# Extra matrix products into fresh PSUM banks ahead of the recurrence's pairwise products and the feed-forward's first feature tile

## The chip, the cores and the metric

The kernel runs on one NeuronCore of a Trainium2 chip. The metric is the device time of one execution in microseconds (us). The engines in the text are TensorE (PE in the profile; its weight loads are PEld), VectorE (DVE), ScalarE (ACT), GpSimd (POOL) and SyncE (SP, which only issues transfers here).

## The reference: one step of a two-layer hybrid encoder

There are 1152 tokens of width 1024: one prompt of 1024 tokens and eight samples of 16 tokens. Everything is f32.

- Layer 0: RMS norm with adaptive shift and scale, then an RWKV-7 time mixing with 16 heads of 64. The recurrence is, per head and token, `S = S*w + (S a) b^T + v k^T`, `y = S r`. Then a SwiGLU feed-forward with 2816 features: `(silu(h Wg) * (h Wu)) Wd`.
- Layer 1: norm, attention of each 64-token chunk to itself and the eight chunks before it, then the same kind of feed-forward.

Outputs are the activations of all tokens, the recurrence's states and the shared keys and values.

## The kernel before

Activations lie with features on the partitions and tokens along the free dimension. A dense product in high precision is three products of a reduced f32 type (fp32r): the operand is split into a high part (ScalarE copy, L268) and a low part (VectorE subtraction, L269), and `mm3` (L271) issues high by high, high by low and low by high. Each product by `mm` (L138) goes through L139, so in the profile nearly all TensorE rows have that line and are told apart by their tiles. A product of two plain f32 operands is issued as two matmul instructions, one of fp32r as one.

**Layer 0's mixing.** Tokens are cut in three blocks of 384 and nine windows of 128 (`w` = 0 to 8, three for a block; window 8 holds the samples). `layer0a` (L1184) weaves the windows of block b-1 with the projections of block b (`proj_lora` at L570 among them), five steps of one to four of the other; the last three windows are woven with the output projection. `win_prep` (L813) works on one window and one half `hf` of the heads. It loads the operands XL and BK by seven transfers (BK has a single buffer, L823), and for each of two chunks `c` takes two PSUM banks `Gs` (L838, tag G, two banks in all) and makes eight pairwise products `G<-XL,BK`: four features by two heads `e`, head 0 on partitions 0 to 63 and head 1 on 64 to 127, each 64 rows by 128 columns of weights with 128 moving columns, head e into bank e. VectorE masks each bank into YL and XL (L845, L847). Then BK is transposed (L856) by way of two more G banks `pt` (L850) and ScalarE copies them out (L858). So one call makes 16 pairwise products and 16 transposes, and there are 18 calls. `win_first`, `win_solve`, `win_merge` and `win_state` do the triangular inverse and the recurrence, on small tiles with the tags st and Y.

**Feed-forward.** Gate and up projections use Strassen's scheme with seven products of half-size operands (`gate_up`, L1319). The tokens are two column groups: c=0 has 512 tokens and moving widths of 256, c=1 has 640 tokens and widths of 320. Product i takes the weight halves (hi, lo) from a generator, takes a wide PSUM tile of two banks (tags S, two buffers, and PT, one buffer) and issues 12 matmuls for each c. The inputs `B[c][i]` come from `strassen_in` (L1255): GpSimd combinations, ScalarE and VectorE splits. For the first of 22 feature tiles, `ffn` (L1361) calls `gate_up` for c=0 (L1365), runs what is left of `strassen_in` for c=1, and calls `gate_up` again for c=1 with the same weights (L1368). The other 21 feature tiles do both c at once (L1370). This happens in both layers.

**What sets the order.** The program text gives priorities; a scheduler that simulates the timeline (L1935) fixes, when the kernel is built, one order of instructions for each engine. At run time each engine works through its own order and waits by semaphores.

Of the kernel before, what the change touches and what calls it, by code (L numbers as in the profile page):

```python
# [137 lines left out]
def mm(nc, out, lhsT, rhs, start, stop):  # L138
    return nc.tensor.matmul(out, lhsT, rhs, start=start, stop=stop)  # L139


class Trunk:
# [631 lines left out]
    def st(self, tag, shape, bufs=1, dt=F32):  # L774
        return self.pp.tile(shape, dt, tag=tag, name=self.nm(tag), bufs=bufs)

    def win_first(self, w, hf, ld):

        nc = self.nc
        b, wi = divmod(w, 3)  # L780
        fs = slice(4 * hf, 4 * hf + 4)
        pa = self.wt("pa", [128, 2, 8, 64], 1)
        for i, n in enumerate(("kk", "b")):
            nc.sync.dma_start(pa[:, i], self.sp[b][n][:, wi, fs, :].rearrange("p f (c t) -> p (f c) t", t=64))
        G = self.bank("G", 2)
        for c in range(2):
            for f in range(4):
                for e in range(2):
                    h = slice(64 * e, 64 * e + 64)
                    mm(nc, G[h, (c * 4 + f) * 64:(c * 4 + f + 1) * 64], pa[h, 1, 2 * f + c], pa[h, 0, 2 * f + c], True, True)  # L790
        aab = self.wt("Aab", [128, 8, 64], 2)
        gv = G.rearrange("p (g t) -> p g t", t=64)
        if w == 8:
            nc.vector.tensor_tensor(aab, gv, self.C("mas").rearrange("p (o t) -> p o t", o=1).broadcast_to([128, 8, 64]), ALU.mult)
        else:
            nc.scalar.activation(aab, gv, AF.Copy)
        for e in range(2):
            nc.scalar.dma_start(ld[:, hf, e], aab[64 * e:64 * e + 64])
        return aab
# [13 lines left out]
    def win_prep(self, w, hf):  # L813

        nc = self.nc
        smp = w == 8
        b, wi = divmod(w, 3)
        fs = slice(4 * hf, 4 * hf + 4)
        R = Ctx()
        src = lambda n, p0=0, p1=128: self.sp[b][n][p0:p1, wi, fs, :].rearrange("p f (c t) -> p (f c) t", t=64)  # L820
        ring, nr = (self.st, 1) if (w, hf) == (7, 1) and 1 else (self.wt, 3)
        xl = ring("XL", [128, 3, 8, 64], nr)
        bk = self.wt("BK", [128, 8, 2, 64], 1)  # L823
        nc.sync.dma_start(xl[0:64, 0], src("kk", 0, 64))
        nc.sync.dma_start(xl[64:128, 1], src("kk", 64, 128))
        nc.sync.dma_start(bk[0:64, :, 0, :], src("b", 0, 64))
        nc.sync.dma_start(bk[64:128, :, 0, :], src("k", 64, 128))
        nc.sync.dma_start(bk[0:64, :, 1, :], src("k", 0, 64))
        nc.sync.dma_start(bk[64:128, :, 1, :], src("b", 64, 128))
        nc.sync.dma_start(xl[:, 2], src("r"))  # L830
        R.eend = self.eends[b][:, fs, 2 * wi:2 * wi + (8 if smp else 2)]
        bkv = bk.rearrange("p (f c) s t -> p f c (s t)", c=2)

        yl = ring("YL", [128, 2, 2, 4, 64], nr)
        mr = self.C("mrs" if smp else "mr").rearrange("p (o t) -> p o t", o=1).broadcast_to([128, 4, 64])
        ma = self.C("mas" if smp else "ma").rearrange("p (o t) -> p o t", o=1).broadcast_to([128, 4, 64])
        for c in range(2):
            Gs = [self.bank("G", 2) for _ in range(2)]  # L838
            for f in range(4):
                for e in range(2):  # L840
                    h = slice(64 * e, 64 * e + 64)
                    mm(nc, Gs[e][:, f * 128:(f + 1) * 128], bkv[h, f, c], xl[h, e:3:2 - e, 2 * f + c, :], True, True)
            for e in range(2):
                gv = Gs[e].rearrange("p (f x t) -> p f x t", f=4, x=2)
                nc.vector.tensor_tensor(yl[:, c, e], gv[:, :, 1, :], mr, ALU.mult)  # L845
                h2 = slice(64 * (1 - e), 64 * (1 - e) + 64)
                nc.vector.tensor_tensor(xl[h2, e, c::2], gv[h2, :, 0, :], ma[h2], ALU.mult)  # L847

        bkt = ring("BKT", [128, 2, 2, 256], nr)
        pt = [self.bank("G", 2) for _ in range(2)]  # L850
        for c in range(2):
            for f in range(4):
                for e in range(2):
                    o0 = (c * 4 + f) * 64
                    h = slice(64 * e, 64 * e + 64)
                    nc.tensor.transpose(pt[e][:, o0:o0 + 64], bkv[h, f, c], self.C("ident")[h, h])  # L856
        for e in range(2):
            nc.scalar.activation(bkt[:, :, e], pt[e].rearrange("p (c f d) -> p c (f d)", c=2, f=4), AF.Copy)  # L858
        R.xl, R.yl, R.bkt, R.TT = xl, yl, bkt, self.TT.pop((w, hf))
        uv = R.uv = self.wt("UV", [128, 2, 2, 4, 64], 3)  # L860
        for c in range(2):
            for e in range(2):
                p0 = 64 * (1 - e)
                nc.sync.dma_start(uv[p0:p0 + 64, c, e], self.sv[b][wi, c * 64:(c + 1) * 64, e, 4 * hf:4 * hf + 4, :])
        return w, hf, R
# [450 lines left out]
        yield put(a21)  # L1316
        yield put(a22)

    def gate_up(self, sd, B, W, cs):  # L1319

        nc = self.nc
        dve = nc.vector
        gp = nc.gpsimd
        n0, n1 = 256 * cs[0], 576 if cs[-1] else 256
        new = (lambda: self.halfraw()[:, :n1]) if n1 == 256 else (lambda: self.ev("t")[:, n0:n1])

        def product(i):
            hi, lo = next(W)
            t = self.wide()[:, 256:832]
            for c in cs:  # L1330
                z = (t[:, 0:256], t[:, 256:576])[c]
                for k in range(4):
                    s = slice(k * 128, (k + 1) * 128)
                    self.mm3(z, hi[:, s], lo[:, s], B[c][i][0][:, k], B[c][i][1][:, k], k == 0, k == 3)
            return t[:, n0:n1]

        def add(eng, out, x, y):
            eng.tensor_tensor(out, x, y, ALU.add)  # L1338

        t1, s0, s1, t5, u2, u3 = (new() for _ in range(6))  # L1340
        nc.scalar.activation(t1, product(0), AF.Copy)
        add(dve, s0, product(1), t1)
        nc.scalar.activation(s0, s0, AF.Silu)
        nc.scalar.activation(s1, product(2), AF.Copy)
        nc.scalar.activation(t5, product(4), AF.Copy)  # L1345
        add(dve, u2, product(5), t1)
        add(gp, s1, s1, t5)
        add(gp, s1, s1, u2)
        self.silu = nc.scalar.activation(s1, s1, AF.Silu)
        add(dve, u3, product(6), u2)  # L1350
        add(gp, t5, t5, u3)
        dve.tensor_tensor(s1, s1, t5, ALU.mult)
        add(dve, u3, product(3), u3)
        dve.tensor_tensor(s0, s0, u3, ALU.mult)
        for h, s in enumerate((s0, s1)):
            for c in cs:
                o, n = 256 * c - n0, (256, 320)[c]
                t0 = 512 * c + n * h
                nc.sync.dma_start(sd[:, t0:t0 + n], s[:, o:o + n])

    def ffn(self, l, B, W, part1, xsrc, dst, done):  # L1361

        nc = self.nc
        sd = [self.dp.tile([128, 2, 1152], F32, name=f"sd{l}_{p}") for p in range(11)]
        self.gate_up(sd[0][:, 0], B, iter(W), (0,))  # L1365
        for _ in part1:
            pass
        self.gate_up(sd[0][:, 0], B, iter(W), (1,))  # L1368
        for f in range(1, 22):
            self.gate_up(sd[f // 2][:, f % 2], B, self.strassen_weights(l, f), (0, 1))  # L1370
        self.ada = self.ada_steps(range(12, 28), "acc", 1) if l == 0 else iter(())
# [2 lines left out]
        act, W = {}, {}  # L1374
# [11 lines left out]
        for p, c in [(p, c) for p in range(9) for c in range(2)] + [(9, 1), (10, 1), (9, 0), (10, 0)]:  # L1386
# [6 lines left out]
                for n in range(8):  # L1393
                    ns = slice(n % 4 * 128, (n % 4 + 1) * 128)
                    d, parts = self.pz(c)
                    for z, o, m in parts:
                        for i in range(2):
                            wh, wl = W[p][i][n // 4]
                            hi, lo = (act[p, c][h][:, i, o:o + m] for h in range(2))
# [553 lines left out]
```

## Time and profile before

| | us |
|---|---|
| three runs: median (lowest, highest) | 3859.59 (3859.28, 3872.24) |
| the profiled execution, its own time | 3864.46 |
| its span, first to last instruction | 3862.7 |
| TensorE busy in the span | 3540.6 |
| VectorE busy | 2291.8 |
| ScalarE busy | 1575.7 |
| mean granted TensorE clock | 0.932 |

Rows of the timeline read: start, duration, engine, line, operation, out<-in, weights' rows*columns, moving shape, count, and in brackets the idle time before it with what ended that. Where a row merges several instructions, the duration runs to the end of the last one. Rows of the windows view read: from:to, length, busy time of PE, PEld, DVE, ACT and POOL with their counts, granted TensorE clock (1.00 is full), mean busy share of the DMA engines, GB/s.

### The profile page before, as it was taken

The numbers are of one execution on the slowest core, as the hardware profiler recorded it, in microseconds if no ns is written. First come the engines' busy times: TensorE is split into PE (matmuls) and PEld (weight loads), VectorE is DVE, ScalarE is ACT, GpSimd is POOL, SyncE is SP. The second block draws the span as 40 slices with busy tenths as digits, with TensorE's granted clock in tenths as the row PEclk, the third lists the DMA queues.
The fourth block names the chain that finished last, engine by engine and source line by source line (L and its number), as shares of the span: only waits on it lengthen the run. The fifth ranks groups of instructions, "written<-read, shape, count | busy, mean of one in ns | idle before, by whom it ended". The sixth has DMA issues, their size and how long they took to land.

```text
span 3862.7 us, 72343 instructions
## 1 busy us (share of the span) xinstructions
PE 3540.6 (92%) x28614; PEld 3125.0 (81%) x28614; DVE 2291.8 (59%) x4420; ACT 1575.7 (41%) x2998; POOL 643.2 (17%) x564
## 2 busy tenths in 40 slices
PE   5889989989888699999999899789889799999999
PEld 4777778777666599999887879677777799999998
DVE  4666666765445764554456752666675764554567
ACT  5545646544223433333311353565654533333310
POOL 0000000000010364453000100000000254453000
PEclk8887998889798789999999999899999899999999
DMA  5775776776664412223755112454555322222521
GB/s 209 233 218 163 214 207 182 200 199 199 187 201 147 143 67 75 74 75 105 254 179 182 70 62 97 141 152 140 153 185 167 116 80 75 74 75 92 171 86 70
DMA packets 428963, 552.31 MB, mean 143 GB/s; under 512 B 128432, under 2 KB 296880, under 8 KB 424144
## 3 DMA queue, kind: packets, MB, share of 16 engines
q1 hardware_dynamic: 352640, 449.49, 36.4%
q0 software_dynamic: 21840, 79.31, 6.8%
q10 hardware_dynamic: 54144, 18.89, 2.1%
q8 instruction: 225, 3.69, 0.4%
q14 instruction: 114, 0.93, 0.1%
HBM read 413.42 MB, written 134.12 MB: 142 GB/s over the span
## 4 chain that ended last, share of the span: by engine, by line
PE 69%; DMA 9%; DVE 9%; issue 6%; ACT 5%; POOL 1%; SPq 1%; ACTq 0%; DVEq 0%; POOLq 0%
PE S L139 31%; PE PT L139 15%; PE acc L139 13%; PE st L139 3%; PE O L139 2%; PE G L139 1%; DVE h L269 1%; PE PT L1779 1%; PE aux L139 1%; DMA raw<-in_wada 1%; DMA TT<-Z 1%; DMA Z<-T 1%; DVE wlo L269 1%; PE Y L139 1%; ACT pts L1780 1%
## 5 line engine op out<-in xcount | busy, mean ns | idle before, releaser
L139 PE MATMUL S<-h,w 128*128 128x320 f32 (+1 forms) x4944 | 698.9, 300 | 18.2 <-DVE h L269 7.7
L139 PEld LDWEIGHTS S<-h,w 128*128 128x128 f32 x4944 | 676.8, 192 | 26.6 <-DVE h L269 12.8
L139 PE MATMUL acc<-mx,whi 128*128 128x384 f32 x1728 | 512.5, 374 | 41.8 <-ACT mx L268 20.2
L139 PE MATMUL S<-h,wh 128*128 128x320 f32 (+1 forms) x2844 | 529.8, 337 | 14.0 <-DVE h L1151 8.1
L139 PEld LDWEIGHTS S<-h,wh 128*128 128x128 f32 x2844 | 455.4, 189 | 70.6 <-issue 11.7
L139 PEld LDWEIGHTS acc<-mx,whi 128*128 128x128 f32 x1728 | 340.4, 205 | 74.1 <-ACT mx L268 23.9
L268 ACT ACTIVATE w<-rq 128x512 fp32r<-128x512 f32 x308 | 192.4, 629 | 503.5 <-PE S L139 203.1
L269 DVE TENSOR_TENSOR w<-rq,w 128x512 fp32r<-128x512 f32 x308 | 268.6, 875 | 199.5 <-ACT w L268 198.9
L139 PE MATMUL PT<-h,w 128*128 128x320 f32 (+1 forms) x2448 | 355.4, 300 | 14.1 <-ACT w L268 6.9
L139 PEld LDWEIGHTS PT<-h,w 128*128 128x128 f32 x2448 | 337.9, 192 | 17.8 <-ACT w L268 7.1
L139 PE MATMUL acc<-mx,wlo 128*128 128x384 f32 x864 | 318.8, 369 | 6.5 <-DVE wlo L269 6.5
L139 PE MATMUL PT<-h,wh 128*128 128x320 f32 (+1 forms) x1428 | 286.4, 344 | 10.8 <-DVE wh L269 3.9
L1338 POOL TENSOR_TENSOR t<-t,t 128x576 f32<-128x576 f32 (+1 forms) x132 | 216.5, 1641 | 417.0 <-ACT t L1345 295.3
L139 PEld LDWEIGHTS PT<-h,wh 128*128 128x128 f32 x1428 | 233.5, 190 | 41.7 <-issue 6.0
L269 DVE TENSOR_TENSOR wlo<-raw,whi 128x1024 fp32r<-128x1024 f32 x114 | 139.6, 1226 | 85.3 <-ACT whi L268 84.3
L139 PEld LDWEIGHTS acc<-mx,wlo 128*128 128x128 f32 x864 | 176.7, 205 | 16.3 <-DVE wlo L269 10.3
L269 DVE TENSOR_TENSOR h<-h,h 128x1024 fp32r<-128x1024 f32 (+4 forms) x112 | 122.9, 1111 | 89.9 <-ACT h L268 73.0
L268 ACT ACTIVATE wh<-rq 128x512 fp32r<-128x512 f32 x124 | 74.8, 625 | 242.8 <-PE S L139 160.7
L268 ACT ACTIVATE h<-h 128x1024 fp32r<-128x1024 f32 (+4 forms) x112 | 103.3, 935 | 168.1 <-DMA h<-sd 111.7
L268 ACT ACTIVATE whi<-raw 128x1024 fp32r<-128x1024 f32 x114 | 119.6, 1053 | 124.3 <-PE acc L139 78.9
L1338 DVE TENSOR_TENSOR t<-S,t 128x576 f32<-128x576 f32 (+1 forms) x116 | 86.4, 745 | 132.0 <-PE S L139 132.0
L1405 DVE TENSOR_TENSOR h<-h,S 128x640 f32<-128x640 f32 (+1 forms) x150 | 111.9, 750 | 78.8 <-PE S L139 78.7
(433 smaller groups left out, 5754.7 us busy)
## 6 DMA issues: line engine op xcount, KB each, us to landing
h<-in_wada SPq DMA_DIRECT2D x64, 512.0 KB, 6.4
rq<-in_wg SPq DMA_DIRECT2D x88, 256.0 KB, 2.6
rq<-in_wu SPq DMA_DIRECT2D x88, 256.0 KB, 2.6
rq<-in_wd SPq DMA_DIRECT2D x88, 256.0 KB, 3.0
raw<-in_wada POOLq DMA_DIRECT2D x32, 512.0 KB, 5.0
kc<-in_ck SPq DMA_DIRECT2D x16, 1024.0 KB, 5.0
vc<-in_cv SPq DMA_DIRECT2D x16, 1024.0 KB, 5.8
sd<-t SPq DMA_DIRECT2D x88, 160.0 KB, 1.9
```

The costliest lines, as they stand in the source:

```text
L139: return nc.tensor.matmul(out, lhsT, rhs, start=start, stop=stop)
L268: self.nc.scalar.activation(hi, x, AF.Copy)
L269: self.nc.vector.tensor_tensor(lo, x, hi, ALU.subtract)
L1338: eng.tensor_tensor(out, x, y, ALU.add)
L1405: nc.vector.tensor_tensor(y, y, d, ALU.add)
L1779: nc.tensor.transpose(pt[:, j * 128:(j + 1) * 128], P[:, j * 128:(j + 1) * 128], self.C("ident"))
L1780: nc.scalar.activation(pts[:, 0:nk * 128], pt[:, 0:nk * 128], AF.Copy)
```

## The change

`keep` is a new function that issues, n times, one f32 product of constants into each of two banks: 64 rows by 128 columns of weights, 512 moving columns, head half e into bank e. `win_prep` calls it for windows 0, 3 and 6: before the pairwise products of each chunk (once, in window 6 twice) into the banks `Gs`, and once before the transposes into `pt`. In `gate_up` a new argument makes each of the seven products begin with one (c=0) or three (c=1) fp32r products of the weights with themselves, 128 rows by 128 columns with 512 moving columns, into the bank of the wide tile which the product itself uses next. Only the first feature tile of each layer passes that argument. The real products that follow start their banks anew, so nothing that is computed changes.

```diff
+    def keep(self, ts, n):
+        for _ in range(n):
+            for e, t in enumerate(ts):
+                h = slice(64 * e, 64 * e + 64)
+                mm(self.nc, t, self.cst[h, 0:128], self.cst[h, 0:512], True, True)
...
         for c in range(2):
             Gs = [self.bank("G", 2) for _ in range(2)]
+            if w % 3 == 0:
+                self.keep(Gs, 1 + (w == 6))
...
         pt = [self.bank("G", 2) for _ in range(2)]
+        if w % 3 == 0:
+            self.keep(pt, 1)
...
-    def gate_up(self, sd, B, W, cs):
+    def gate_up(self, sd, B, W, cs, keep=0):
...
             hi, lo = next(W)
-            t = self.wide()[:, 256:832]
+            t = self.wide()
+            for _ in range(keep):
+                mm(nc, t[:, 512 * cs[0]:512 * cs[0] + 512], hi[:, 0:128], hi, True, True)
+            t = t[:, 256:832]
...
-        self.gate_up(sd[0][:, 0], B, iter(W), (0,))
+        self.gate_up(sd[0][:, 0], B, iter(W), (0,), 1)
         for _ in part1:
             pass
-        self.gate_up(sd[0][:, 0], B, iter(W), (1,))
+        self.gate_up(sd[0][:, 0], B, iter(W), (1,), 3)
```

That is 44 f32 products in `win_prep` (22 pairs: 6 for window 0, 6 for window 3, 10 for window 6) and 28 fp32r products in each layer's feed-forward.

## The prediction, before the run

> **What bounds the kernel now.** I read the page first, then windows of 50 us over the span, then windows of 0.1 us around each change of the granted clock, then TensorE's timeline there. From the page:
>
> ```profile
> span 3862.7 us, 72343 instructions
> PE 3540.6 (92%) x28614; PEld 3125.0 (81%) x28614; DVE 2291.8 (59%) x4420; ACT 1575.7 (41%) x2998; POOL 643.2 (17%) x564
> PEclk8887998889798789999999999899999899999999
> PE 69%; DMA 9%; DVE 9%; issue 6%; ACT 5%; POOL 1%; SPq 1%; ACTq 0%; DVEq 0%; POOLq 0%
> ```
>
> TensorE is busy for 92% of the span and carries 69% of the chain that ended last; but the clock row shows that a busy TensorE is not always a fast one. Between the edges found with the 0.1 us windows:
>
> ```profile
> 347.90:365.00 17.10, 16.96 (x60) 12.29 (x59) 16.06 (x33) 12.37 (x23) 0.53 (x1) 0.50 0.56 176
> 368.40:399.10 30.70, 29.47 (x392) 25.69 (x391) 20.17 (x42) 11.60 (x22) 1.58 (x3) 0.50 0.66 173
> 665.30:702.90 37.60, 35.94 (x154) 28.81 (x151) 31.57 (x75) 22.22 (x39) 1.05 (x2) 0.50 0.57 167
> 979.40:1016.90 37.50, 31.61 (x170) 22.38 (x168) 21.20 (x58) 7.04 (x13) 1.42 (x3) 0.50 0.65 173
> 1337.80:1375.30 37.50, 29.32 (x94) 23.30 (x95) 34.06 (x54) 18.26 (x40) 29.91 (x25) 0.55 0.11 35
> 3068.30:3082.00 13.70, 6.11 (x27) 5.82 (x28) 13.70 (x38) 11.35 (x23) 0.08 (x1) 0.50 0.00 0
> 3099.00:3110.00 11.00, 9.54 (x34) 7.90 (x35) 9.39 (x13) 1.99 (x5) 7.84 (x7) 0.53 0.00 0
> 1400.00:1450.00 50.00, 50.00 (x379) 50.00 (x378) 26.64 (x30) 16.61 (x28) 24.80 (x16) 1.00 0.21 73
> ```
>
> The third number is TensorE's busy time, the fifth VectorE's, the seventh GpSimd's, then the clock. The clock here is half or full and nothing between (0.55 is a mean over an edge). Half-clock stretches last 17.1, 30.7, 37.6 and 37.5 us, which is 5, 9, 11 and 11 times 3.41 to 3.42 us: it is decided anew every 3.4 us or so. The first three window stretches are no idle time: in 665.30 to 702.90 TensorE is busy for 35.94 of 37.60 us and still runs at 0.50. The change sits at exactly these places: `win_prep` of windows 0, 3 and 6 (from 328.85, 662.65 and 976.72 us) and the feed-forwards' first feature tiles (from 1321.92 and 3059.51 us). The last row is what every later feature tile looks like: full clock, TensorE never idle; nothing is to be had there.
>
> Why does a busy TensorE lose its clock? The timeline, mostly of window 3 (the last two rows are the first products of window 6 and of layer 1's feed-forward):
>
> ```profile
> 662.65 0.48 PE L139 MATMUL G<-XL,BK 64*128 64x128 f32 x2
> 663.06 0.69 PE L139 MATMUL st<-TT,p 32*32 32x32 f32 x16
> 663.68 1.16 PE L139 MATMUL G<-XL,BK 64*128 64x128 f32 x14
> 664.76 1.53 PE L139 MATMUL st<-TT,p 32*32 32x32 f32 x32
> 679.84 3.06 PE L139 MATMUL G<-XL,BK 64*128 64x128 f32 x16 [1.01 <-DMA BK<-sp_k]
> 684.41 2.07 PE L139 MATMUL G<-XL,BK 64*128 64x128 f32 x8
> 707.58 1.16 PE L139 MATMUL G<-XL,BK 64*128 64x128 f32 x8
> 976.72 1.16 PE L139 MATMUL G<-XL,BK 64*128 64x128 f32 x8
> 3059.51 5.67 PE L139 MATMUL S<-h,w 128*128 128x256 f32 x24 [2.17 <-ACT w L268]
> ```
>
> The 3.4 us before the fall at 665.3 hold little but products on 32 or 64 of the 128 rows with 32 or 128 moving columns. So what seems to count is how much of the array is in use, not whether an instruction runs. Weighting each instruction's moving columns by its share of the 128 rows, and f32 twice against fp32r, I counted by hand some 2,900 columns for that interval, and put the point at which the clock falls near 3,100 (an estimate from the rows of this trace). Once at half clock an interval has room for only half as many, so with such a mix the clock can hardly come back.
>
> **The change part by part.** It removes and moves nothing. *Price of a pair in `win_prep`.* A pair is four instructions of 512 moving columns on 64 rows, two for each half of the array. The nearest rows:
>
> ```profile
> 328.85 1.16 PE L139 MATMUL G<-XL,BK 64*128 64x128 f32 x16
> 329.94 0.45 PE L139 MATMUL acc<-mx,wlo 128*128 128x384 f32 x1
> 952.03 1.12 PE L139 MATMUL st<-y,cst 128*128 128x512 f32 x2
> 953.09 0.64 PE L139 MATMUL aux<-raw,scT 128*32 128x256 f32 x8
> ```
>
> Sixteen instructions of 128 columns, both halves alternating, take 329.94 - 328.85 = 1.09 us at full clock. That is as many columns as a pair has (16 x 128 = 4 x 512), so a pair costs 1.09 us where its halves overlap. At 707.58 eight instructions, of one half alone, take as long (1.16 with the tail), so a pair whose halves come apart costs 2.2 us. The two instructions of 512 columns at 952.03 need 1.06 us and agree. At half clock: 3.0 us for 16 as at 679.84, 4.0 us apart (twice the row of 684.41). By the count above a pair adds 2 x 2 x 512 x 2 x 1/2 = 2,048, so one pair lifts the interval before 665.3 from 2,900 to well over 3,100. The pairs need only constants and a free G bank, so they can run while BK is still in flight.
>
> *Window 0* (6 pairs). Its first call runs in 328 to 341 us at full clock, where TensorE has no idle time: three pairs cost 3 x 1.09 = 3.3 us (6.6 apart). Its second call lies in 347.9 to 365.0, where VectorE is busy for 16.06 of 17.10 us. At full clock TensorE would need 8.5 us there and the pairs fit in, but only 1.0 us can be gained before VectorE is the bound. The stretch from 368.4 follows a wait:
>
> ```profile
> 346.07 0.44 PE L139 MATMUL acc<-ag,whi 128*128 128x384 f32 x1 [1.44 <-ACT e L605]
> 366.85 1.13 PE L139 MATMUL G<-XL,BK 64*128 64x128 f32 x8 [1.74 <-DMA BK<-sp_k]
> 995.85 2.04 PE L139 MATMUL G<-XL,BK 64*128 64x128 f32 x8 [5.07 <-DMA BK<-sp_k]
> ```
>
> The wait at 366.85 belongs to window 1, which gets no extra product, and a TensorE that is early waits longer there. So of the 30.70 - 20.17 = 10.5 us that VectorE would allow I take 4 (ends 0 and 10.5). Sum for window 0: +3.3 - 1.0 - 4 = -1.7 us, between +6 and -8.
>
> *Window 3* (6 pairs, in 662 to 693 us). All of the 37.6 us stretch has them in it. At full clock TensorE needs 18.0 us and 6 pairs x 1.09 to 2.2 = 6.5 to 13 us, so VectorE's 31.57 us is what is late next: at most 6.0 us. I take 4, since VectorE is never quite full and one pair ahead of 665 stands in the open: -4 us.
>
> *Window 6* (10 pairs, in 976 to 1018 us). The two pairs ahead of each chunk can use the wait of 5.07 us at 995.85 for BK. TensorE: 31.61 / 2 = 15.8 us, plus 10.9 us of pairs (22 apart), 26.7 to 37.8 us against 37.5; VectorE has only 21.20. So the gain lies between 10.8 and 0 us; I take 6.
>
> *Feed-forward, layer 0.* One fp32r product of 512 columns is bounded by
>
> ```profile
> 1321.92 5.46 PE L139 MATMUL S<-h,w 128*128 128x256 f32 x24 [2.46 <-DVE kk L329]
> 1328.78 3.30 PE L139 MATMUL S<-h,w 128*128 128x256 f32 x24
> 1331.92 1.60 PE L139 MATMUL PT<-h,w 128*128 128x256 f32 x12
> 1333.98 1.70 PE L139 MATMUL S<-h,w 128*128 128x256 f32 x12 [0.47 <-ACT rq L1345]
> ```
>
> (1331.92 - 1328.78) / 24 = 0.131 us for 256 columns, so 0.26 us for 512 at full clock, twice that, 0.5, at half. For c=0 TensorE is dense from 1321.92 on, the first extra product needs a PSUM tile that is free only then, and the clock comes back during its first 24 matmuls (5.46 us against 3.30) either way: 7 x 0.26 = +1.8 us in the open. For c=1, 21 x 0.26 = 5.5 us lie in the stretch 1337.8 to 1375.3, where TensorE waits for the low parts; at full clock TensorE would need 29.32 x 0.55 + 5.5 = 21.6 us there, against 34.06 on VectorE and 29.91 on GpSimd. Late next is VectorE: 37.5 - 34.06 = 3.4 us at most, and I take that. Sum -1.6 us. Were the clock not held, the 21 products would cost 0.5 us each, 10.5 us against 8.2 us of idle time.
>
> *Feed-forward, layer 1.* For c=0, 7 x 0.26 = 1.8 us (3.5 at half clock) partly fall in 3068.3 to 3082.0, where VectorE is busy for all of 13.70 us and TensorE for 6.11; for c=1, 3099 to 3110 can shrink from 11.0 to VectorE's 9.39. +1.8 - 1.6, about 0 (-2 to +3).
>
> Sum: -1.7 - 4 - 6 - 1.6 + 0 = -13.3 us. The profiled execution took 3864.46 us (span 3862.7 and 1.8 around it): 3851.2. The median of the runs, 3859.59, is 4.9 below that execution, so in terms of the median 3846 us.
>
> No engine but TensorE gets an instruction, no transfer is added, and no semaphore wait but that for the bank, which the real product needs too. Queued behind a waiting extra product are all later TensorE instructions, as they were behind the real one.
>
> **The rivals.** *All of it passes on.* If VectorE's queue has room outside the stretches, each stretch shrinks to VectorE's busy time: -8.2 (window 0: +3.3 - 1.0 - 10.5), -6, -10.8, -1.6, -1.6 = -28 us, 3831. For it: the chain is TensorE's for 69%. Against: 16.06 of 17.10 and 34.06 of 37.50 us on VectorE.
>
> *The clock does not follow.* If idle time alone decides, the extra products buy nothing in the windows, where the longest waits ahead of `win_prep`'s products are 1.44, 1.01 and 5.07 us, and are paid at half clock: 3.3 us for window 0's first three, 19 pairs x 3.0 = 57 us for the others, less those waits of 7.5 us: +53, 3912 us. It decides if 665 to 703 us still shows 0.50. Against it is the row of 665.30: 35.94 us busy, clock 0.50.
>
> The Trainium skill, "TensorE: Matmul & The Clock Gate", section "Why this matters for your kernels", has a rule of this kind: no idle gaps over about 3 us between matmul bursts, since one idle window halves the clock. By it this rival would hold for windows 0 and 3; the trace does not agree, with 35.94 of 37.60 us busy at 0.50.
>
> *Nothing is left.* Added instructions shift the scheduler's simulated timeline, so that it may order other work anew, and each later loss of clock falls elsewhere; the gain is then lost to later waits: 3856 to 3866. For it: between 300 and 1250 us TensorE waits for many different producers, none of which the change touches:
>
> ```profile
> PE st L139 <- ACT y L1056: 10.9, 4, 7.6
> PE st L139 <- DVE t L900: 9.9, 12, 4.0
> PE G L139 <- DMA BK<-sp_k: 7.8, 3, 5.1
> ```
>
> (total us, times, longest us).
>
> **How the numbers follow.** A measurement of this kernel can tell about 0.5%, 19 us, from no change: faster is below 3840, slower above 3879. Chances: forecast 0.48 (3838 to 3855), all passes on 0.27, nothing left 0.15, clock does not follow 0.10. Faster: 0.27 and 0.07 of the forecast's lower edge, 0.34. Slower: 0.10 and 0.02 for pairs that come apart in window 6, 0.12. Same: 0.54. The range goes from 3818 (the second case, with 13 us for a better order) to 3872 (the third and part of window 6 at the price of pairs apart); left out are mainly the 3912 case and half its way.
>
> **What would show it.** Right: clock near 1.00 in the stretches of windows 3 and 6 and of c=1 in both layers, VectorE above 90% there, pairs of about 1.1 us; the stretch of window 1 still partly at 0.50. Wrong: 0.50 as before (second rival), pairs at 2.2 us or more, or a stretch shorter than VectorE's busy time in it, which would mean that VectorE was not what is late next.

## The result and the profile after

| | median us | lowest to highest | runs |
|---|---|---|---|
| before | 3859.44 | 3858.65 to 3872.24 | 4 |
| after | 3908.96 | 3896.08 to 3921.58 | 4 |

The ratio is 1.0121, with an interval of 1.0096 to 1.0145: the change costs 1.2%, about 49 us. The forecast was 3846 us and the range ended at 3872. The profiled execution of after is its slowest (3921.58), so its trace shows 57 us of loss.

From the page of after (span, busy times, clock, shares of the chain that ended last):

```profile
span 3919.4 us, 72636 instructions
PE 3589.8 (92%) x28758; PEld 3144.3 (80%) x28758; DVE 2296.6 (59%) x4420; ACT 1572.7 (40%) x2998; POOL 641.4 (16%) x564
PEclk8887989698789689999999999999999899999999
PE 67%; DMA 11%; DVE 9%; issue 6%; ACT 5%; POOL 1%; SPq 1%; ACTq 0%; DVEq 0%; POOLq 0%
```

TensorE is busy 49 us longer, and the clock row is no better than before. The feed-forward's first product of layer 0 stood at 1321.92 us before; after, it stands at 1386.95. That is 65 us later, more than the whole loss of this execution, so all of it arises before the feed-forward. The stage from 320 us on, before and then after (columns as in the windows view above):

```profile
320.00:1321.92 1001.92, 892.38 (x9579) 726.77 (x9578) 617.56 (x1374) 462.87 (x899) 83.40 (x136) 0.86 0.65 187
```
```profile
320.00:1386.95 1066.95, 946.37 (x9687) 749.67 (x9684) 619.72 (x1374) 459.96 (x901) 83.82 (x137) 0.84 0.61 175
```

TensorE's busy time grew by 54 us and its idle time by 11 us (1066.95 - 946.37 = 120.6, against 109.5). What became of the half-clock stretches of before, and three stretches that after has in their place (windows view of after):

```profile
347.90:365.00 17.10, 15.42 (x50) 9.87 (x48) 15.06 (x32) 9.26 (x18) 0.53 (x1) 0.60 0.65 162
368.40:399.10 30.70, 30.13 (x459) 24.25 (x459) 15.56 (x30) 13.85 (x29) 0.53 (x1) 0.50 0.33 101
665.30:702.90 37.60, 33.89 (x228) 24.73 (x228) 24.79 (x66) 19.18 (x36) 2.53 (x5) 0.86 0.48 123
351.00:403.00 52.00, 51.37 (x561) 38.27 (x559) 32.16 (x64) 23.01 (x47) 1.06 (x2) 0.51 0.36 105
692.00:754.00 62.00, 61.18 (x573) 46.38 (x573) 36.19 (x69) 26.89 (x52) 2.11 (x4) 0.50 0.38 112
1037.00:1089.00 52.00, 49.26 (x208) 33.05 (x210) 10.75 (x23) 8.86 (x18) 1.59 (x3) 0.51 0.49 130
```

In 665 to 703 us the clock is back (0.86 for 0.50), but the half-clock time has only moved: it now lies in 692 to 754, and it is longer. The reader should see what stands at its beginning. TensorE's timeline of after:

```profile
330.65 1.13 PE L139 MATMUL G<-cst 64*128 64x512 f32 x4
331.62 1.06 PE L139 MATMUL G<-XL,BK 64*128 64x128 f32 x16
350.53 2.39 PE L139 MATMUL G<-cst 64*128 64x512 f32 x4 [1.62 <-ACT BKT L869]
356.91 2.07 PE L139 MATMUL G<-cst 64*128 64x512 f32 x2
358.78 1.91 PE L139 MATMUL G<-XL,BK 64*128 64x128 f32 x8
691.80 2.33 PE L139 MATMUL G<-cst 64*128 64x512 f32 x4 [3.11 <-ACT BKT L869]
```

At 350.53 and at 691.80 an extra pair is the first instruction of its call, ahead of BK, and TensorE stands still for the bank, which ScalarE's copy of the last transposes still holds. Right there the clock falls. Pairs behind it are paid at half clock: 358.78 - 356.91 = 1.87 us for one product, where a pair at full clock takes 331.62 - 330.65 = 0.97 us. Not all of the wait is new: at the place of the 1.62 us, TensorE in before stood 1.44 us for ScalarE (346.07, in the prediction's rows; it is a projection that waits there, not a product of `win_prep`).

From this I had three theories. *Blocked*: the extra products are put ahead of BK, TensorE waits for the bank, the clock falls there and the rest is paid at half clock. *Order*: the added instructions shift the scheduler's simulated timeline; the new order of the whole window stage costs, whatever the products are. *Price*: the TensorE time of 22 pairs is lost as such.

### The profile page after: what moved, and what is told of

It is laid out like the page before. It is cut to its first block, busy times and chain, and to the rows that moved or that the text cites. A ratio compares the mean times of both kernels' runs of the same rounds, so it can differ in the third digit from the quotient of the medians.

```text
span 3919.4 us, 72636 instructions
## 1 busy us (share of the span) xinstructions
PE 3589.8 (92%) x28758; PEld 3144.3 (80%) x28758; DVE 2296.6 (59%) x4420; ACT 1572.7 (40%) x2998; POOL 641.4 (16%) x564
## 4 chain that ended last, share of the span: by engine, by line
PE 67%; DMA 11%; DVE 9%; issue 6%; ACT 5%; POOL 1%; SPq 1%; ACTq 0%; DVEq 0%; POOLq 0%
PE S L139 31%; PE PT L139 15%; PE acc L139 11%; PE st L139 3%; PE G L139 2%; PE O L139 2%; DVE h L269 1%; PE PT L1793 1%; PE aux L139 1%; DVE wlo L269 1%; DMA raw<-in_rw_o 1%; ACT pts L1794 1%; DMA sp_k<-rr 1%; PE Y L139 1%; DMA L<-ld 1%
## 5 line engine op out<-in xcount | busy, mean ns | idle before, releaser
L139 PE MATMUL S<-h,w 128*128 128x320 f32 (+1 forms) x4944 | 690.3, 298 | 6.3 <-DVE h L269 6.3
L1352 DVE TENSOR_TENSOR t<-S,t 128x576 f32<-128x576 f32 (+1 forms) x116 | 86.4, 745 | 129.3 <-PE S L139 128.9
```

## The experiments

All differences are between medians, against the kernel before, which was run beside each group (medians 3864.3 to 3868.2 us).

| run | what | difference, us | ratio, interval |
|---|---|---|---|
| ff | feed-forward part alone | +4.6 | 0.9995 to 1.0028 |
| win | window part alone | +45.2 | 1.0092 to 1.0135 |
| narrow | window part, 64 columns | +44.3 | 1.0084 to 1.0130 |
| tied | window part, weights from BK | +54.5 | 1.0113 to 1.0156 |
| w0 | window 0 alone | +41.0 | 1.0081 to 1.0137 |
| w6 | window 6 alone | +38.4 | 1.0060 to 1.0111 |
| held16 | order of win, 16 columns | +29.3 | 1.0051 to 1.0102 |
| nudge_e | no extra product, other order | +34.4 | 1.0056 to 1.0105 |
| nudge_load | no extra product, other order | +13.9 | 1.0016 to 1.0043 |
| inplace | order of before, 22 pairs | +20.4 | 1.0036 to 1.0071 |
| inplace03 | the same, windows 0 and 3 | +17.8 | 1.0031 to 1.0067 |
| best | inplace03, and c=1 in layer 0 | +15.4 | 1.0029 to 1.0063 |
| inplace0 | order of before, window 0 | +5.7 | 1.0001 to 1.0025 |
| inplace3 | order of before, window 3 | 0.0 | 0.9991 to 1.0019 |
| inplace6 | order of before, window 6 | +17.9 | 1.0029 to 1.0061 |
| inpl16 | order of before, 22 pairs of 16 columns | +13.9 | 1.0024 to 1.0047 |
| sep16 | the same, each by its own product | +21.5 | 1.0034 to 1.0066 |
| sep03 | inplace03, each by its own product | +23.2 | 1.0048 to 1.0078 |

### The parts, and three theories: ff, win, narrow, tied

```diff
# ff:      no keep() in win_prep          win: no keep argument in gate_up
# narrow (as win):
-                mm(self.nc, t, self.cst[h, 0:128], self.cst[h, 0:512], True, True)
+                mm(self.nc, t[:, 0:64], self.cst[h, 0:128], self.cst[h, 0:64], True, True)
# tied (as win; W is bkv[:, 0, c], for the transposes bkv[:, 0, 0]):
+                mm(self.nc, t, W[h], self.cst[h, 0:512], True, True)
```

> Only the feed-forward's extra products are left (56 in all: per layer 7 for c=0, 21 for c=1); win_prep is as before. All three theories of the loss (blocked: the window's extra products are put ahead of BK and TensorE then stands at them for the G bank; order: the scheduler's new order of the window stage costs the time whatever the products are; price: the TensorE time of the 22 pairs as such) place it in the windows, so they expect 3853 to 3861 us here, with the half-clock stretches of the first feature tile of layer 0 shorter than the 37.5 us of before. Were the loss in the feed-forward, over 3890.

> Only the window's 22 pairs are left (88 products into G banks), no extra product in the feed-forward. Blocked, order and price all expect the loss here: 3900 to 3920 us, about 4 more than the whole change has. If the two parts only cost something together, 3860 to 3870.

> The window's 22 pairs alone, each product with 64 moving columns instead of 512, so an eighth of the work on TensorE at the same places, with the same waits for a bank. Price expects 3859 + 60/8, 3860 to 3868 us. Order expects the full loss, 3895 to 3915. Blocked expects about half of it, 3875 to 3895: TensorE still stands at the first products for the bank and the clock still falls there, but the pairs that follow at half clock cost an eighth.

> The window's 22 pairs alone, at full size, but with a piece of BK as weights instead of a constant, so that they cannot be put ahead of BK's arrival and stand right before the real products. Blocked expects most of the loss gone: 3850 to 3872 us, and no product on G that waits for ACT's copy of the last transposes for 2 us or more at the start of window 0's second call and of window 3. Order expects 3895 to 3915. Price expects 3895 to 3915 as well, since the columns are the same.

The feed-forward part alone can't be told from no change; the window part alone has the loss. *Blocked*, as the cause of the whole loss, falls with tied: its products can't stand ahead of BK, and it lost no less. That clears the wait for the bank, but not waits in general: in tied TensorE stands 4.10 us for BK at 348.68, and its pairs behind that are paid at half clock too. *Price*, taken alone, falls with narrow, which at an eighth of the columns lost as much as win. Only order had expected that.

In the profiles, win's stage lasts 1051.09 us with 928.60 busy, so 122.5 idle; narrow's, in an execution that was its fastest, 1033.23 with 895.10, so 138.1 idle. Against before's 892.4 and 109.5, win lost more to busy time and narrow nearly all to idle time.

### Holding one order and changing only the products: held16 and inplace

The scheduler fixes each engine's order when the kernel is built; after that, instructions in its list can be replaced or put in without moving another. held16 builds win and then shrinks each of the 88 instructions; inplace builds the kernel before and then puts 88 in.

```diff
# held16 (as win), after the order is fixed:
+    shrink(nc, 16)    # each G<-cst: same place, same waits, 16 moving columns
# inplace (as before), after the order is fixed:
+    extras(nc, t.cst.tensor.name, 512)  # pair ahead of the first real product into its banks, with its waits
```

> The window's pairs alone, in exactly the order of instructions that the kernel with the window's pairs alone has on every engine, but each of the 88 products shrunk after the order was fixed to 16 moving columns, 1/32 of the work; the waits stay. So only the order, and the waits for a bank, can cost. Price expects 0 to +6 us against the kernel before. Order expects +30 to +45, nearly the whole loss. If both count, the accounts of the traces say how much: TensorE's idle time grew by 14 us of the 49 that the window stage lost in the profile of the window's pairs alone, its busy time by 35; then about +14.

> The other half: exactly the order of the kernel before on every engine, and the 44 f32 products (88 instructions) of full size put, after the order was fixed, straight ahead of the first real product into the same bank, with its wait. Order expects 0 to +8 us against the kernel before, or a gain where the clock rises (the prediction's -8). Price expects +35 to +45. If both count by the accounts, about +35. Blocked, which the kernel with a piece of BK as weights speaks against, expects no more than 0 to +10 here, since nothing stands ahead of BK.

In inplace the two products of a pair stand together where their real products are at most ten TensorE instructions apart, else each by its own. Every other matmul keeps its place.

Both count, though 20.4 for inplace was expected neither by a theory alone nor by both together. win's order with shrunk products keeps 29.3 of the 45.2 us; the order of before with full-size products costs 20.4. The windows view of held16, then of inplace, for the stage:

```profile
320.00:1348.07 1028.07, 898.79 (x9658) 733.79 (x9656) 618.01 (x1374) 459.15 (x899) 83.54 (x136) 0.85 0.63 182
```
```profile
320.00:1335.78 1015.78, 900.00 (x9706) 719.81 (x9705) 618.75 (x1375) 460.64 (x901) 83.81 (x137) 0.89 0.64 184
```

held16's loss in this execution is idle time: 129.3 us against 109.5, with only 6.4 more busy. In inplace the clock is up (0.89 for 0.86), as the prediction wanted, yet the stage is 14 us longer. Shrinking to 16 columns doesn't make a product free, though; that comes below.

### One window at a time with the scheduler's own order: w0 and w6

```diff
-            if w % 3 == 0:
+            if w == 0:        # w6: if w == 6 (both places; no keep in gate_up)
```

> Only window 0 gets its 6 pairs, as the change does it; the order after it is as far from before as with all 22 (some 6,400 of 22,300 matmul instructions elsewhere, by comparing the two lists). Order expects +30 to +45 us, as with all. Price expects 6/22 of the loss, +10 to +14.

> Only window 6 gets its 10 pairs; some 1,400 matmul instructions stand elsewhere than before, all after window 6. Price expects 10/22 of the loss, +18 to +22 us, since these 10 pairs lie in a half-clock stretch. Order expects less than window 0 alone: 0 to +15.

Six pairs cost 41 us, ten cost 38, all twenty-two 45. Price alone would have them add up. w6 went against both theories as I had sized them: with a fifth as many instructions moved it still lost 38. Part of that is the pairs themselves: in the order of before, below, window 6's pairs cost 17.9 us and window 0's 5.7. If the two parts simply add, which wasn't tested, the new order costs some 20 us in w6 and 35 in w0.

### A new order without any extra work: nudge_e and nudge_load

```diff
# nudge_e
-                for e in range(2):
+                for e in (1, 0) if w == 0 else (0, 1):
# nudge_load
+        if w == 0:
+            nc.sync.dma_start(xl[:, 2], src("r"))     # first of the seven, not last
...
-        nc.sync.dma_start(xl[:, 2], src("r"))
+        if w != 0:
+            nc.sync.dma_start(xl[:, 2], src("r"))
```

> The kernel before, without any extra product; only the text of window 0 issues the pairwise products of head 1 ahead of those of head 0. The work is the same, instruction for instruction, but the scheduler makes a new order of it: some 5,100 of 22,300 matmul instructions stand elsewhere, about as many as with the change. If leaving the order of before costs by itself, +20 to +40 us. If the order costs only where the extra products stand in it, -5 to +8.

> The kernel before, without any extra product; only the text of window 0 issues the transfer of r as the first of the seven and not as the last. The work is the same; some 3,600 of 22,300 matmul instructions stand elsewhere. If leaving the order of before costs by itself, +15 to +40 us. If the order costs only where the extra products stand in it, -5 to +8.

This is the plainest experiment of the study. The same instructions in another order cost 34 and 14 us. nudge_e's stage, and its longest waits on TensorE, with the same four of before behind them (waits view: total us, times, longest):

```profile
320.00:1344.67 1024.67, 874.27 (x9532) 715.82 (x9531) 615.62 (x1373) 457.49 (x897) 77.36 (x136) 0.85 0.64 183
```
```profile
PE acc L139 <- ACT mx L268: 19.5, 5, 9.5
PE G L139 <- DMA pa<-sp_b: 15.2, 4, 6.9
PE acc L139 <- ACT whi L268: 12.7, 5, 5.5
PE G L856 <- DVE XL L847: 10.5, 5, 4.8
```
```profile
PE acc L139 <- ACT mx L268: 15.1, 4, 9.4
PE G L139 <- DMA pa<-sp_b: 4.1, 1, 4.1
PE acc L139 <- ACT whi L268: 5.0, 2, 4.4
PE G L856 <- DVE XL L847: 4.0, 4, 2.2
```

TensorE idles 150.4 us in place of 109.5, and is busy 18 us less. No one wait carries it: the four shown grew by 4.4, 11.1, 7.7 and 6.5 us. The stage is 22.8 us longer; the other 12 us of this execution's loss come behind it. Two other orders are few: whether the order of before is an uncommonly good one wasn't tested.

### The order of before, window by window: inplace03, best, inplace0, inplace3, inplace6

```diff
# as inplace, with
-                    if f == 0 and w % 3 == 0:
+                    if f == 0 and w in (0, 3):    # inplace0: w == 0, inplace3: w == 3, inplace6: w == 6
# best, besides: 3 products of hi ahead of each of the seven first products for c=1 of layer 0
```

> The order of before, held, with the 12 pairs of windows 0 and 3 put straight ahead of the first real product into the same bank, none in window 6. By the trace of the kernel with all 22 put so, the projections stood 4 to 6 us earlier than before by 850 to 970 us, and all of the loss came after 979 us, in window 6: so -4 to -6 us against the kernel before, half-clock time at 347 to 399 and 665 to 703 us about half of what it was. If price counts, 12/22 of the +20 that all 22 cost so: +11.

> The last kernel, and in layer 0's feed-forward the 21 extra products for c=1 put in the same way, in the order of before; none for c=0, none in layer 1. The first feature tile took 2.9 us less with the change's extra products there, 1.8 us of products for c=0 in the open included: so another -3 to -5 us, -7 to -11 in all. If price counts, +11 or more.

> The order of before, held, with window 0's 6 full-size pairs alone. By the prediction's step for window 0, -1.7 us (-8 to +6). By the price alone, +6 to +9. If a shift costs whichever it is, +12 to +20.

> The order of before, held, with window 3's 6 full-size pairs alone. By the prediction's step for window 3, -4 us (-6 to 0), with the clock of 662 to 703 us near 0.9. By the price alone, +6 to +9. If a shift costs whichever it is, +12 to +20.

> The order of before, held, with window 6's 10 full-size pairs alone, straight ahead of the real products and so behind the arrival of BK. By the prediction's step for window 6, -6 us (-10.8 to 0). By the trace with all 22 put so, where 979 to 1041 us held 47.8 us at half clock in place of 37.5 and the window ended 16 to 20 us later, +15 to +20.

inplace03 and best missed: +18 and +15, no gain. inplace3 is the run that tests the prediction's mechanism by itself. Its stretch of window 3 and its pairs there (windows view, then timeline):

```profile
665.30:702.90 37.60, 32.08 (x217) 23.34 (x215) 34.72 (x82) 22.22 (x40) 1.58 (x3) 0.95 0.65 186
```
```profile
663.06 1.13 PE L179 MATMUL G<-cst 64*128 64x512 f32 x4
664.02 0.38 PE L179 MATMUL G<-XL,BK 64*128 64x128 f32 x2
679.24 1.81 PE L179 MATMUL G<-cst 64*128 64x512 f32 x3 [1.46 <-DMA BK<-sp_k]
```

The clock is 0.95 where it was 0.50, a pair takes 0.96 us, and VectorE is busy for 34.72 of 37.60 us, 92%, as the prediction said. How much of that is a gain needs a comparison beyond before. ff has nothing added in any window and, as far as the traces show, the TensorE order of before up to 1321 us; so it is a second execution of before's windows. Its stretch, and its first product of window 3:

```profile
665.30:702.90 37.60, 33.23 (x154) 26.97 (x154) 32.70 (x78) 22.25 (x38) 1.59 (x3) 0.64 0.63 178
```
```profile
661.55 0.48 PE L139 MATMUL G<-XL,BK 64*128 64x128 f32 x2
```

Three landmarks of TensorE's tiles, in before, in inplace3 and (two of them) in ff; first and last start are the two times in each row:

```profile
L139 PE MATMUL G<-XL,BK x576: 272/272/580, 328.9 to 1159.1; 64*128 64x128 f32 x192
L139 PE MATMUL acc<-rr,whi x48: 334/522/690, 102.7 to 708.9; 128*128 128x384 f32 x48
L139 PE MATMUL Y<-XL,ssv x256: 206/206/227, 1116.4 to 1239.9; 64*64 64x16 f32 x128
```
```profile
L179 PE MATMUL G<-XL,BK x576: 269/272/579, 331.2 to 1157.0; 64*128 64x128 f32 x192
L179 PE MATMUL acc<-rr,whi x48: 333/443/689, 103.3 to 706.5; 128*128 128x384 f32 x48
L179 PE MATMUL Y<-XL,ssv x256: 206/206/227, 1114.5 to 1240.8; 64*64 64x16 f32 x128
```
```profile
L139 PE MATMUL G<-XL,BK x576: 271/272/579, 331.6 to 1157.3; 64*128 64x128 f32 x192
L139 PE MATMUL acc<-rr,whi x48: 337/522/690, 103.1 to 706.1; 128*128 128x384 f32 x48
```

From window 3's first TensorE instruction (an extra product in inplace3) to the last acc<-rr,whi it takes 46.3 us in before (from 662.65), 44.6 in ff and 43.4 in inplace3 (from 663.06). So in these executions the pairs won 1 to 3 us there, their own price paid. Over all windows nothing of that is to be seen: the pairwise products take 825.8 us from first to last in inplace3, 4.4 less than in before, but 825.7 in ff, so that difference isn't the pairs' doing. And being early doesn't last: inplace3 stands 2.1 us ahead of before at 1157 us and 0.9 behind at the recurrence's last product on Y (1240.8 against 1239.9). What follows waits for the recurrence's output (inplace3, timeline; before has 7.59 us at 1247.71), and that didn't come earlier.

```profile
1248.50 2.07 PE L179 MATMUL st<-y,cst 128*128 128x512 f32 x2 [7.48 <-ACT y L1106]
```

Window 6 is the other way. inplace6, timeline, and the stretch that was at 0.50 throughout in before:

```profile
999.14 3.75 PE L179 MATMUL G<-cst 64*128 64x512 f32 x4 [5.09 <-DMA BK<-sp_k]
1002.69 1.91 PE L179 MATMUL G<-XL,BK 64*128 64x128 f32 x8
```
```profile
979.40:1016.90 37.50, 31.60 (x177) 19.69 (x176) 18.83 (x53) 6.37 (x12) 1.04 (x2) 0.75 0.57 162
```

Here too the clock is up in the stretch (0.75), since window 6's first call ran at full speed. But held to the order, the products of the second call wait for BK with everything else (5.09 us), and right behind that wait two products take 1002.69 - 999.14 = 3.55 us at half clock. The ten products of that call, from 999 to 1039 us, take about 17 us in this way, about as much as the kernel lost.

### What the instructions cost without their columns: inpl16, sep16, sep03

```diff
# inpl16, sep16 (as inplace)
-    extras(nc, t.cst.tensor.name, 512)
+    extras(nc, t.cst.tensor.name, 16)
# sep16, sep03 (each product straight ahead of its own real product, with that one's wait alone)
-            if b - a <= 10:
+            if b - a <= 0:
```

> The order of before, held, with all 22 pairs put in straight ahead of the first real product, but each of 16 moving columns. If the TensorE time of the products is what costs in the held order, 0 to +4 us against the kernel before. If the 88 added instructions and the waits that they take over cost, or if any shift of TensorE against the other engines does, +12 to +20.

> The order of before, held, 88 instructions of 16 moving columns as in the last kernel of that size, but each product straight ahead of its own real product, so that no instruction waits earlier than before. If the earlier waits cost the 14 us, 0 to +4 us against the kernel before. If the added instructions as such cost, or any shift, +10 to +18 again.

> The order of before, held, the 12 full-size pairs of windows 0 and 3, each product straight ahead of its own real product, so that the two halves of the array mostly come apart (1.06 us a product at full clock) and no instruction waits earlier. If the earlier waits made the +18 of the twelve pairs, -4 to +6 us. If their price does, +13 to +25.

The pairs of 16 columns cost 14 us, those of 512 cost 20. The earlier waits, which I had suspected, are cleared: without them it was 21 in sep16 and 23 in sep03, which has the pairs of inplace03. A small product isn't as cheap as its columns (inpl16, timeline):

```profile
332.15 0.40 PE L179 MATMUL G<-cst 64*128 64x16 f32 x4
332.39 1.14 PE L179 MATMUL G<-XL,BK 64*128 64x128 f32 x16
980.14 0.61 PE L179 MATMUL G<-cst 64*128 64x16 f32 x4
980.61 1.13 PE L179 MATMUL G<-XL,BK 64*128 64x128 f32 x8
```

A pair takes 0.24 us, or 0.47 at 980, a quarter of a full one and not 1/32: 22 pairs make 5 to 10 us. That is short of 14 to 21. One place seems to show more: window 6 in before, then in sep16:

```profile
979.40:1042.00 62.60, 53.73 (x409) 38.63 (x409) 29.44 (x76) 15.05 (x30) 3.69 (x7) 0.65 0.67 178
```
```profile
979.40:1042.00 62.60, 57.08 (x392) 43.03 (x391) 26.85 (x70) 11.46 (x23) 2.64 (x5) 0.56 0.61 171
```

The clock is lower there (0.56 for 0.65), but that is no sign of the small products. inplace0, which has nothing added in window 6, shows the same:

```profile
979.40:1042.00 62.60, 56.27 (x420) 40.86 (x418) 31.02 (x78) 15.31 (x31) 3.49 (x7) 0.56 0.69 184
```

ff has 0.61 there and inplace3 0.59, so the difference lies within what executions of one order show. Where the rest of the 14 to 21 us comes from stays open.

The account, then. Of the window part's 45 us, 29 remain with win's order and shrunk products, and 16 go with their size. Of the 29, the small products themselves are 5 to 10 us by their rows, or 14 to 21 by what they cost in the order of before. That leaves 8 to 24 us for the order, with the waits for the bank that belong to it, beside 14 and 34 for two orders with no product added. It is an estimate: it takes the parts to add up, and each difference is uncertain by some us. No version beat the kernel before; the nearest, window 3's pairs alone in its order, came out even.

## Why the prediction was wrong

**The order.** The sum goes wrong at its first step: it laid the extra products into the timeline of before. They are 144 more instructions for a scheduler that orders by simulated time, and it put thousands of others elsewhere. The rival *Nothing is left* named this, but priced it at 3856 to 3866, as if a new order could only take back the gain. Two orders without any extra product cost 14 and 34 us, and the window part's own order some 8 to 24 by the account above. That term was put at nothing in the sum and mis-sized in the rival; either of the two measured ones is larger than the 13.3 us of the whole forecast gain.

**The bank wait.** "Queued behind a waiting extra product are all later TensorE instructions, as they were behind the real one" is wrong: needing no BK, the extra product is put where the real one couldn't stand, and waits there (1.62 and 3.11 us at 350.53 and 691.80). But tied shows that without this wait the loss is as large.

**Why the clock falls.** Right in the main. With the order held, 6 pairs bring 665 to 703 us to 0.95 (0.86 in inplace, 0.91 in inplace03, 0.77 in best, which came there 6 us later), with TensorE busy for less than before; without full-size pairs there it is 0.50 to 0.68 (before, inplace6, ff, inplace0), and with pairs of 16 columns at the same places 0.55 and 0.59 (inpl16, sep16). So it seems to be the columns that raise it, not the added instructions; but where the halves came apart, in sep03, full-size products left it at 0.70. What the prediction had wrong is that the stretch was a fixed one: in ff the same instructions in the same order lost the clock near 672.7 us, not at 665.3. The figure of 3,100 columns wasn't tested. *The clock does not follow* fell, since its own sign, 0.50 in this stretch, didn't come, although its 3912 us is close to what was measured. The Trainium skill, "TensorE: Matmul & The Clock Gate", section "Why this matters for your kernels", speaks of idle gaps over about 3 us. The fall at 692 in after, behind a wait of 3.11 us, would agree with it; 0.50 in before against 0.95 in inplace3 in window 3, with no wait above 1.5 us in either, isn't explained by it.

**Price of a pair.** Right at full clock: 0.97 us for 1.09. At half clock it is less than I took: 3.55 us for two products apart, for 4.0.

**Window 0**, -1.7 with ends of +6 and -8: +5.7 in the order of before, at the unfavourable end. Its second call's stretch, 347.9 to 365.0 us, at 0.50 in before, was at 0.91 in ff without any extra product, so the time at half clock that was to be won there isn't in every execution.

**Window 3**, -4: 0.0 for the kernel, with an interval of -3.5 to +7.3 us. The stretch itself gave 1 to 3 us, less than the 4, and VectorE was nearly full there (92%), as I said. The step that failed is that a gain there was carried to the end: the recurrence's last product on Y, at 1240 us, came no earlier.

**Window 6**, -6 with ends of 0 and -10.8: +17.9 in the order of before. "The two pairs ahead of each chunk can use the wait of 5.07 us" failed there: straight ahead of the real products they stand behind BK's arrival, and pay half clock. With an order of the scheduler's own it was +38.

**Feed-forward.** Layer 0, -1.6. The rows are of the first long run of the following tile in before and in ff:

```profile
1393.34 3.36 PE L139 MATMUL PT<-h,w 128*128 128x256 f32 x24
```
```profile
1390.52 3.36 PE L139 MATMUL PT<-h,w 128*128 128x256 f32 x24
```

2.8 us earlier, from a start at the same time (1321.92 and 1321.99): right in sign in this one execution, a little small. Layer 1, 0: in ff its feed-forward starts 4.0 us later than in before (3063.50 against 3059.51) and the span ends 5.8 later (3868.5 against 3862.7), so +1.8, within -2 to +3. The 2.8 us didn't reach that far: 6.8 us were lost in between, where ff has nothing added.

**All of it passes on** fell: the most that any version passed on was inplace3's 0.0.

## What to carry to other kernels

Where a scheduler orders a kernel by simulated time, an edit of a few instructions is also a new order of the whole stage, and here that alone cost 14 to 34 us; price it as a term of its own, with both signs, and test a change twice, once as the scheduler lays it and once with the old order held. A faster clock in one stretch is worth only what the chain that ends the stage gets of it: inplace3 was 2 us ahead at 1157 us and no longer at 1241. Look at a second execution of the same order before you credit a change with a few us: a trace without any extra product showed the same lead. And a number that comes out near the measured one doesn't make its mechanism right.

## What was not expected of the hardware

A matmul pair cut from 512 to 16 moving columns still took 0.24 us for 0.97, a quarter. In the order of before, 88 such instructions cost 14 to 21 us, against 5 to 10 us of their own time on TensorE; that remains unexplained. And where the clock falls isn't fixed by the order of instructions: over window 3's stretch it was 0.50 in before and 0.64 in ff, over window 0's second call 0.50 and 0.91, with the same TensorE instructions in the same order.
